# Seven block products in place of eight in half of the last matrix's contraction, with partial sums added by DMA and the residual kept in DRAM

## The chip, the core and the metric

One core of a Trainium2 chip runs the whole kernel. Its time is the device time of one execution in microseconds (us); the number compared is the median of several executions. Five engines work side by side, each through its own list of instructions in order: PE (TensorE, the matmuls), DVE (VectorE), ACT (ScalarE), POOL (GpSimd) and SP (SyncE, which here only issues transfers). They meet at semaphores. An instruction that waits holds up everything behind it on its own engine.

## The reference

One decoder layer on 256 positions with 2048 channels, all in float32:

```
u   = rms_norm(x)
o   = diff_attention(q, k, v of u)  +  conv module(u),  each times a sigmoid gate of u
h   = x + rms_norm(o @ w_out)
ff  = square(relu(rms_norm(h) @ w_ff1)) @ w_ff2      # 2048 -> 8192 -> 2048
out = h + rms_norm(ff)
```

The change is in the last product, `@ w_ff2`: 256 rows, a contraction over 8192, 2048 columns.

## The kernel before

**Precision.** Every weight and activation is kept as a rounded part (hi) and the rest (lo), both in the type float32r. A product is three matmuls: hi by hi, hi by lo, lo by hi. All weights come from DRAM as chunks of 128 x 2048 float32 (1 MB), loaded on SP's queue into `raw`. ACT casts a chunk to `wh` (L103), and DVE subtracts to get `wl` (L109). There are three buffers each of `raw`, `wh` and `wl`. `done()` after a chunk's last matmul frees a pair of `wh`, `wl`, and `fill()` then writes down the load and the split of the chunk three further on, so the cast of chunk i+3 waits for the last matmul of chunk i.

**Two ways to multiply.** `ws_pair` (L175 to L184) holds a piece of weight on PE and streams the activations: per chunk 16 matmuls of 512 columns and 16 of 256. `as_part` and `as_block` (L190 to L215) hold a piece of activation and stream the weight: per chunk 4 x 2 x 3 = 24 matmuls of 512 columns.

**Stages.** The convolution's input product runs to about 240 us, the heads with q, k, v and attention to 530, gates, convolution output and `w_out` to 840. Then comes the feed-forward part in four quarters q of its 8192 middle channels: 16 chunks of `w_ff1` with `ws_pair` (16 groups of middle channels are squared and split into the tiles `g`), then 16 chunks of `w_ff2` with `as_block`, for each of four blocks n of 512 columns four chunks kc. The sums of a block land in two PSUM banks and are copied to `acc` by ACT in quarter 0 (L658) and added to it by DVE afterwards (L660). Two tiles `ps` of two banks each take turns; four more banks (`psx`) serve everything else.

**Start.** The first two chunks are multiplied while they arrive. Meanwhile ACT and DVE form the squares of x, PE sums them over the partitions into `aux`, and ACT and DVE make `rb`, the row factors 1/rms (L217 to L219, called at L347). Every convolution pair's sum `z` (two buffers) is multiplied by `rb` at L391, so until `rb` is there the sums are parked in `z` and the PSUM tiles behind them stay full.

**Order of work.** A scheduler lays each engine's list out from the program text, its priorities (`high_priority`) and its own estimates, except where `pin` keeps program order. So an edit in one place can move instructions elsewhere.

Of the kernel before, what the change touches and what calls it, by code (L numbers as in the profile page):

```python
# [18 lines left out]
P = 128  # L19
# [26 lines left out]
EARLY = 3  # L46

# [5 lines left out]
def tile_layer(ctx, tc, x, x_t, pre, vecs, lams, rope_t, subln, b_conv, post_mix, post_ff,  # L53
# [9 lines left out]
    psx = ctx.enter_context(tc.tile_pool(name="psx", bufs=1, space=PSUM))  # L63
# [11 lines left out]
    for q in range(NQ):  # L75
        order += [w_f1[q * KT + ct] for ct in range(KT)]
        order += [w_f2[n, q * 4 + kc] for n in range(NB) for kc in range(4)]
    queue = []
    state = {"next": 0, "live": 0}

    pin = tc.keep_in_program_order

    def load(pieces):
        i = state["next"]
        state["next"] += 1
        state["live"] += 1
        chunk = (rawp.tile([P, CHUNK], F32, name="raw"), whp.tile([P, CHUNK], F32R, name="wh"),
                 wlp.tile([P, CHUNK], F32R, name="wl"))
        for j in range(pieces):
            load_part(chunk, i, j, pieces)  # L90
        queue.append(chunk[1:])
        return chunk
# [19 lines left out]

    def fill():
        while state["live"] < WBUFS and state["next"] < len(order):
            pieces = 4 if state["next"] in (n_mix, n_mix + 1, n_mix + 3) else 1
            chunk = load(pieces)
            w = CHUNK // pieces
            for j in range(pieces):
                split_hi(chunk, j * w, (j + 1) * w)
                split_lo(chunk, j * w, (j + 1) * w)  # L120

# [39 lines left out]

    def new_ps():
        return psm.tile([P, 2, 512], F32, name="ps")
# [36 lines left out]
    def as_block(acts, stagger=False, apart=False):  # L200
        ps = new_ps()
        pss = [ps[:, 0], aux_ps()] if apart else [ps[:, t] for t in range(NT)]
# [58 lines left out]
    lead = [load(0) for i in range(2)]  # L261

# [6 lines left out]
    load_x(0, 2)  # L269
    load_w(1, 0, nc.scalar)  # L270
    load_w(0, 0)
    pin(nc.scalar.dma_start(gpre, pre))
# [4 lines left out]
    for j in range(2, 4):  # L277
# [15 lines left out]
    mask = const.tile([P, S], F32, name="mask")  # L293
    nc.gpsimd.memset(mask, 0.0)
    nc.gpsimd.affine_select(mask[:, P:S], mask[:, P:S], pattern=[[-1, P]], compare_op=ALU.is_ge,
                            fill=NEG_INF, base=0, channel_multiplier=1)

# [54 lines left out]
    rope_sb = const.tile([P, 2, S], F32, name="rope_sb")  # L352
    pin(nc.sync.dma_start(rope_sb, rope_t))
    sub8 = const.tile([P, VD], F32, name="sub8")
    pin(nc.sync.dma_start(sub8, subln.partition_broadcast(P)))
    lam_in = const.tile([P, 4, HD], F32, name="lam_in")
    pin(nc.sync.dma_start(lam_in, lams.partition_broadcast(P)))

# [6 lines left out]
    tmpp = mid.enter_context(tc.tile_pool(name="tmpp", bufs=2))  # L365
    y_all = lnp.tile([P, KT, S], F32, name="y_all")
# [197 lines left out]
    gpool = ctx.enter_context(tc.tile_pool(name="gpool", bufs=KT // 2))  # L564
    pmx = fin.tile([P, D], F32, name="pmx")
    nc.gpsimd.dma_start(pmx, post_mix.partition_broadcast(P))
    y_sb = fin.tile([P, NT, D], F32, name="y_sb")
    h_sb = fin.tile([P, NT, D], F32, name="h_sb")
    nc.gpsimd.dma_start(h_sb, x_r)
# [5 lines left out]
    for n in range(NB):  # L575
        ps = as_block(ma, apart=(n == NB - 1))
        ns = slice(n * 512, (n + 1) * 512)
        with tc.high_priority(offset=CHAIN if n == NB - 1 else 0):
            for t in range(NT):
                sq = fin2.tile([P, 512], F32, name="fsq")  # L580
# [14 lines left out]
    def square(t, n):  # L595
        sq = fin2.tile([P, 512], F32, name="fsq")
# [18 lines left out]
    with tc.high_priority(offset=CHAIN):  # L615
        third = load(4)
        pin(nc.vector.reciprocal(r1[:, 0:1], r1[:, 0:1]))
# [18 lines left out]
    pff = pmx  # L636
    nc.gpsimd.dma_start(pff, post_ff.partition_broadcast(P))
# [3 lines left out]
    r3 = fin.tile([P, NT], F32, name="r3")  # L641
    for q in range(NQ):
        ga = Act(gpool, "g")
        for j in range(KT // 2):
# [4 lines left out]
            gg = fin2.tile([P, 2, S], F32, name="gg")  # L649
            nc.vector.scalar_tensor_tensor(gg, z, 0.0, z, op0=ALU.max, op1=ALU.mult)  # L650
            ga.put_pair(j, gg)
        for n in range(NB):
            ps = as_block(ga, stagger=(q == NQ - 1 and n == NB - 1), apart=(q == NQ - 1 and n == NB - 1))
# [92 lines left out]
```

## Time and profile before

| | |
|---|---|
| median of 3 runs | 1552.69 us (1552.65 to 1554.11) |
| profiled execution, its own time | 1552.62 us |
| span of its profile | 1550.9 us |
| instructions | 19142 |
| mean granted TensorE clock | 0.998 |
| PE, DVE, ACT busy, share of the span | 99%, 72%, 46% |

The span runs from the first to the last instruction; 1.7 us of the execution's own time lie outside it. Busy shares say how much an engine worked, not whether the others waited for it: that is read from what its instructions waited for.

### The profile page before, as it was taken

Reading aid. Unit: us, or ns where it says so; the run is one execution under the profiler, and the core shown is the slowest. Engines: PE = TensorE matmul, PEld = TensorE weight load, DVE = VectorE, ACT = ScalarE, POOL = GpSimd, SP = SyncE. Lnnn points to the kernel's source line nnn. Section 1 sums busy time; section 2 is a strip of 40 time slices with the busy share of each in tenths; the row PEclk is TensorE's granted clock in tenths of the full one; section 3 lists DMA queues with packets and bytes.
Section 4 is the critical chain, followed back from the end, with each engine's and each line's share of the span. In section 5 each row is a group of like instructions: output and inputs, shape, how many; then the busy total and the mean of one; then the engine's idle time right before and its main releaser. Section 6 shows DMA issues by size and latency. Waiting matters only on the chain.

```text
span 1550.9 us, 19142 instructions
## 1 busy us (share of the span) xinstructions
PE 1537.6 (99%) x7830; PEld 1314.2 (85%) x7830; DVE 1116.3 (72%) x1399; ACT 717.4 (46%) x743; POOL 5.1 (0%) x28
## 2 busy tenths in 40 slices
PE   9999999999999999999999999999999999999997
PEld 8888888888888888888887888888888888888886
DVE  7999999999999997966546764456545664466554
ACT  7444454645555545733446443444333443344442
POOL 0000000000000000000000000000000000000000
PEclk9999999999999999999999999999999999999999
DMA  8655555454545555555754655555455555555552
GB/s 304 218 191 188 188 190 187 165 188 163 190 163 187 193 201 192 179 200 180 270 196 156 225 188 185 191 210 188 173 195 209 190 190 180 198 193 190 187 193 82
DMA packets 45143, 296.86 MB, mean 191 GB/s; under 512 B 5120, under 2 KB 5248, under 8 KB 10368
## 3 DMA queue, kind: packets, MB, share of 16 engines
q1 hardware_dynamic: 43920, 289.61, 52.9%
q0 software_dynamic: 704, 5.24, 0.8%
q8 instruction: 61, 1.00, 0.3%
q10 hardware_dynamic: 432, 0.79, 0.2%
q14 instruction: 26, 0.21, 0.0%
HBM read 293.53 MB, written 2.10 MB: 191 GB/s over the span
## 4 chain that ended last, share of the span: by engine, by line
PE 99%; DVE 1%; ACT 0%; issue 0%; POOL 0%; DVEq 0%; ACTq 0%; POOLq 0%
PE ps L180 29%; PE ps L196 16%; PE ps L197 16%; PE ps L198 16%; PE ps L182 15%; PE ps L168 1%; PE po L463 1%; PE ps L171 1%; PE s L435 0%; PE aux L299 0%; PE aux L197 0%; PE aux L196 0%; PE aux L198 0%; DVE y_sb L679 0%; PE s L434 0%; PE aux L557 0%
## 5 line engine op out<-in xcount | busy, mean ns | idle before, releaser
L109 DVE TENSOR_TENSOR wl<-raw,wh 128x2048 fp32r<-128x2048 f32 (+2 forms) x292 | 625.0, 2144 | 368.0 <-ACT wh L103 363.9
L103 ACT CAST wh<-raw 128x2048 fp32r<-128x2048 f32 (+2 forms) x292 | 522.0, 1793 | 716.5 <-PE ps L198 352.2
L180 PE MATMUL ps<-act,wh 128*128 128x512 f32 x1984 | 478.9, 392 | 0.1
L180 PEld LDWEIGHTS ps<-act,wh 128*128 128x128 f32 x1984 | 364.3, 188 | 70.7 <-PE ps L182 0.3
L182 PEld LDWEIGHTS ps<-act,wl 128*128 128x128 f32 x1984 | 256.6, 191 | 10.1
L182 PE MATMUL ps<-act,wl 128*128 128x256 f32 x1984 | 263.8, 284 | 0.0
L196 PE MATMUL ps<-wh,act 128*128 128x512 f32 x624 | 243.9, 391 | 0.0
L197 PE MATMUL ps<-wl,act 128*128 128x512 f32 x624 | 243.4, 390 | 0.0
L198 PE MATMUL ps<-wh,act 128*128 128x512 f32 x624 | 243.3, 390 | 0.0
L380 DVE SCALAR_TENSOR_TENSOR y_all<-c,vec,y_all 128x256 f32<-128x256 f32 x480 | 209.1, 479 | 0.0
L196 PE MATMUL ps<-wh,g 128*128 128x512 f32 x496 | 193.0, 389 | 0.0
L197 PE MATMUL ps<-wl,g 128*128 128x512 f32 x496 | 193.0, 389 | 0.0
L198 PE MATMUL ps<-wh,g 128*128 128x512 f32 x496 | 192.9, 389 | 0.0
L198 PEld LDWEIGHTS ps<-wh,act 128*128 128x128 f32 x624 | 117.1, 188 | 24.2
L196 PEld LDWEIGHTS ps<-wh,act 128*128 128x128 f32 x624 | 117.2, 188 | 24.1
L197 PEld LDWEIGHTS ps<-wl,act 128*128 128x128 f32 x624 | 117.2, 188 | 23.8
L198 PEld LDWEIGHTS ps<-wh,g 128*128 128x128 f32 x496 | 93.1, 188 | 19.4
L196 PEld LDWEIGHTS ps<-wh,g 128*128 128x128 f32 x496 | 93.1, 188 | 19.2
L197 PEld LDWEIGHTS ps<-wl,g 128*128 128x128 f32 x496 | 93.1, 188 | 19.1
L188 DVE TENSOR_TENSOR z<-z,ps 128x512 f32<-128x512 f32 x64 | 43.5, 679 | 0.0
L187 ACT COPY z<-ps 128x512 f32<-128x512 f32 x64 | 37.5, 586 | 2.4 <-PE ps L182 1.6
L660 DVE TENSOR_TENSOR y_sb<-ps,y_sb 128x512 f32<-128x512 f32 x23 | 14.9, 686 | 20.1 <-PE ps L198 20.1
(172 smaller groups left out, 687.5 us busy)
## 6 DMA issues: line engine op xcount, KB each, us to landing
raw<-in_w_f_dram SPq DMA_DIRECT2D x124, 1024.0 KB, 4.8
raw<-in_w_q_dram SPq DMA_DIRECT2D x16, 1024.0 KB, 4.9
raw<-in_w_k_dram SPq DMA_DIRECT2D x16, 1024.0 KB, 4.8
raw<-in_w_v_dram SPq DMA_DIRECT2D x16, 1024.0 KB, 4.8
raw<-in_w_ga_dram SPq DMA_DIRECT2D x16, 1024.0 KB, 4.8
raw<-in_w_gc_dram SPq DMA_DIRECT2D x16, 1024.0 KB, 4.8
raw<-in_w_co_dram SPq DMA_DIRECT2D x16, 1024.0 KB, 4.8
raw<-in_w_o_dram SPq DMA_DIRECT2D x16, 1024.0 KB, 4.8
```

Source lines behind the costliest of these rows:

```text
L103: i = nc.scalar.copy(wh[:, a:b], raw[:, a:b])
L109: i = (eng or nc.vector).tensor_sub(wl[:, a:b], raw[:, a:b], wh[:, a:b].bitcast(F32))
L168: a = nc.tensor.matmul(ps, wh[:, sl], acts.both(k), start=(k == 0), stop=False)
L171: b = nc.tensor.matmul(ps[:, S:], wl[:, sl], acts.hi(k), start=False, stop=(k == KT - 1))
L180: nc.tensor.matmul(ps[:, j], wh[:, k * P:(k + 1) * P], acts.both(k), start=(k == 0), stop=False)
L182: nc.tensor.matmul(ps[:, j, S:], wl[:, k * P:(k + 1) * P], acts.hi(k), start=False, stop=(k == KT - 1))
L187: nc.scalar.copy(dst, ps[:, :, S:])
L188: nc.vector.tensor_tensor(dst, dst, ps[:, :, 0:S], op=ALU.add)
L196: nc.tensor.matmul(ps, acts.hi(k, a, b), wh[:, sl], start=(k == 0), stop=False)
L197: nc.tensor.matmul(ps, acts.hi(k, a, b), wl[:, sl], start=False, stop=False)
L198: nc.tensor.matmul(ps, acts.lo(k, a, b), wh[:, sl], start=False, stop=(k == KT - 1))
L380: i = nc.vector.scalar_tensor_tensor(y, c[:, j:j + S], vcol(ct, V_DW + j), y, op0=ALU.mult, op1=ALU.add)
```

## The change

**Products.** For seven of the eight pairs of column blocks (all but the second pair in quarter 3; `fast(q, m)`), the chunks kc 0 and 1 of both blocks are multiplied by blocks. The activations of a chunk form 2 x 2 blocks of 128 x 256, the weights of the two blocks of columns 2 x 2 blocks of 256 x 512, and seven products of sums of them take the place of the eight plain ones (Strassen's scheme): 42 matmuls per kc and pair in place of 48. kc 2 and 3 stay plain. The order of the four is `FF_ORDER` = 0, 2, 1, 3. The weight sums are formed by `fast_part` in four parts that carry 12, 12, 12 and 6 matmuls: per kc seven casts of 1024 columns on ACT (L159), seven subtractions (L160) and four additions (L165) of 1024 columns on DVE, in place of two casts and two subtractions of 2048. Both `raw` buffers of the pair stay taken until the fourth part. The activation sums are formed by `put_fast` for the first four groups of each quarter.

**Sums.** A pair of blocks uses all eight PSUM banks (`psx` is closed after the second norm and its banks become the pool `psy`). The scheme's own four banks are drained in mid-pair (one ACT copy, L798, four DVE additions, L800 to L803), the plain ones at the pair's end (four DVE additions, L819 to L822). In quarter 0 they go to `acc` directly, later to a tile `ev` (one buffer), which two DMAs per pair add to `acc` in SBUF (L825): ten DMAs of 512 KB over the five pairs.

**Residual.** `h_sb` (2 MB) is written to a DRAM tensor `h_keep` after the second norm (L730), and its SBUF goes to the new tiles; in quarter 3 it is read back in four pieces (L860), with the last gain (L857).

**Also moved.** `rope_sb`, `sub8`, `lam_in` and `mask` go to another pool, and their loads stand earlier on SP's queue: three rows from 13 on, ahead of a weight chunk, and not three rows from 23 on. The load of `gpre` comes first on ACT's queue, ahead of a weight piece.

```diff
+FAST = 2
+FF_ORDER = (0, 2, 1, 3)
+def fast(q, m):
+    return q < NQ - 1 or m == 0
...
+    def split_sum(wt, half, src):
+        hi, lo = (w[:, half * 1024:(half + 1) * 1024].rearrange("p (a n) -> p a n", a=2) for w in wt)
+        nc.scalar.copy(hi, src)
+        nc.vector.tensor_sub(lo, src, hi.bitcast(F32))
...
+        if part == 0:
+            split_sum(wt, 0, w11)
+            split_sum(wt, 1, new_sum("t1", w11, w12))
+            add(w12, w12, w22)
+        elif part == 1:
+            split_sum(wt, 0, w12)
+            split_sum(wt, 1, new_sum("t2", w12, w11))
+        elif part == 2:
+            split_sum(wt, 0, w21)
+            split_sum(wt, 1, new_sum("t4", sums["t2"], w21))
+        else:
+            split_sum(wt, 0, w22)
+            release_raw(i)
+            release_raw(i + 1)
...
-    load_w(1, 0, nc.scalar)
-    load_w(0, 0)
-    pin(nc.scalar.dma_start(gpre, pre))
+    pin(nc.scalar.dma_start(gpre, pre))
+    load_w(0, 0)
+    load_w(1, 0, nc.scalar)
...
-    rope_sb = const.tile([P, 2, S], F32, name="rope_sb")
-    pin(nc.sync.dma_start(rope_sb, rope_t))
...
+    rope_sb = lnp.tile([P, 2, S], F32, name="rope_sb")
+    pin(nc.sync.dma_start(rope_sb, rope_t))
...
+    nc.gpsimd.dma_start(h_keep, h_sb)
+    hst.close()
+    psx_st.close()
...
+        for kc in FF_ORDER:
+            if kc < FAST:
+                for pair in ((A1, A5), (A7, A6), (A2, A4), (A3,)):
+                    wh, wl = take()
+                    for half, a in enumerate(pair):
+                        ps = own[a] if a in own else shared[a]
+                        for i in range(2):
...
+                            nc.tensor.matmul(ps, g[:, 0, a], wh[:, sl], start=first, stop=False)
+                            nc.tensor.matmul(ps, g[:, 0, a], wl[:, sl], start=False, stop=False)
+                            nc.tensor.matmul(ps, g[:, 1, a], wh[:, sl], start=False, stop=last)
+                    done()
...
+        if q:
+            for t in range(NT):
+                nc.gpsimd.dma_start(acc[:, t, m * 1024:(m + 1) * 1024], ev[:, t].rearrange("p i n -> p (i n)"),
+                                    accum_op=ALU.add)
```

ACT's list at the start of the program, around the two instructions that make the row factors `rb` and `rt` from PSUM. Before:

```order
L187 COPY z<-ps 128x512 [waits PE_49]
L103 CAST wh<-raw 128x2048 [waits DMAHW4_49,PE_49]
L103 CAST wh<-raw 128x2048 [waits DMAHW5_49,DVE_49,PE_49]
L218 ACTIVATE rb<-aux,epsn 128x256 [waits PE_49]
L218 ACTIVATE rt<-aux,epsn 128x2 [waits PE_49]
L103 CAST wh<-raw 128x2048 [waits DMAHW6_49,DVE_49,PE_49]
L392 ACT_TABLE_LOAD [waits DMAHW0_49]
```

With the change:

```order
L278 COPY z<-ps 128x512 [waits PE_49]
L425 ACTIVATE xsq<-xt 128x1024 [waits DVE_49]
L143 CAST wh<-raw 128x2048 [waits DMAHW6_49]
L143 CAST wh<-raw 128x2048 [waits DMAHW7_49,PE_49]
L143 CAST wh<-raw 128x2048 [waits DMAHW0_49,DVE_49,PE_49]
L143 CAST wh<-raw 128x2048 [waits DMAHW1_49,DVE_49,PE_49]
L309 ACTIVATE rb<-aux,epsn 128x256 [waits PE_49]
L309 ACTIVATE rt<-aux,epsn 128x2 [waits PE_49]
```

From the second pair's copy to `rb`, two weight casts stood ahead, and now four do: one has slipped behind that copy, and one that came after `rb` now comes before it, where it waits for PE to free its buffer.

DVE's list at the same place, from the last addition of squares to the first product with `rb`. Before:

```order
L341 TENSOR_TENSOR xss<-xss 128x256 [waits DVE_49]
L109 TENSOR_TENSOR wl<-raw,wh 128x2048 [waits DMAHW5_49,PE_49,Activation_49]
L219 RECIPROCAL rb<-rb 128x256 [waits Activation_49]
L219 RECIPROCAL rt<-rt 128x2 [waits Activation_49]
L391 TENSOR_TENSOR z<-z,rb 128x512 [waits DVE_49]
L391 TENSOR_TENSOR z<-z,rb 128x512
```

With the change:

```order
L429 TENSOR_TENSOR xss<-xss 128x256 [waits DVE_49]
L149 TENSOR_TENSOR wl<-raw,wh 128x2048 [waits DMAHW0_49,PE_49,Activation_49]
L310 RECIPROCAL rb<-rb 128x256 [waits Activation_49]
L310 RECIPROCAL rt<-rt 128x2 [waits Activation_49]
L149 TENSOR_TENSOR wl<-raw,wh 128x2048 [waits DMAHW1_49,PE_49]
L482 TENSOR_TENSOR z<-z,rb 128x512 [waits DVE_49]
L482 TENSOR_TENSOR z<-z,rb 128x512
```

A weight subtraction now stands between the reciprocal and the products with `rb`.

PE's list in the feed-forward part, with buffer numbers, where one chunk of `w_ff2` follows another. Before, in quarter 1 (every chunk boundary there reads like this one):

```order
L197 MATMUL ps_8871<-wl_8805,g_8229 128x512
L198 MATMUL ps_8871<-wh_8804,g_8229 128x512
L196 MATMUL ps_8871<-wh_8834,g_8315 128x512 [waits Activation_49]
L197 MATMUL ps_8871<-wl_8835,g_8315 128x512 [waits DVE_49]
L198 MATMUL ps_8871<-wh_8834,g_8315 128x512
```

With the change, in the second pair of quarter 1, at the end of kc 1 and the start of kc 3 (`wh_9265` is the second part's buffer, `wh_9297` the third's, `wh_9317` the fourth's, `wh_9337` and `wh_9355` the two plain chunks'):

```order
L795 MATMUL ps_9166<-wh_9265,gs_8521 128x512
L794 MATMUL ps_9167<-wl_9298,gs_8432 128x512 [waits DVE_49]
L795 MATMUL ps_9167<-wh_9297,gs_8432 128x512
L793 MATMUL ps_9167<-wh_9297,gs_8521 128x512
L794 MATMUL ps_9167<-wl_9298,gs_8521 128x512
L795 MATMUL ps_9167<-wh_9297,gs_8521 128x512
L794 MATMUL ps_9168<-wl_9318,gs_8432 128x512 [waits DVE_49]
...
L795 MATMUL ps_9168<-wh_9317,gs_8521 128x512
L815 MATMUL ps_9167<-wh_9337,g_8785 128x512 [waits Activation_49]
L815 MATMUL ps_9168<-wh_9355,g_8785 128x512 [waits Activation_49]
L816 MATMUL ps_9167<-wl_9338,g_8785 128x512 [waits DVE_49]
```

The last matmul of the second part (first row) is now followed by only ten others before the first plain chunk's first matmul, and the second plain chunk's first matmul stands right behind that one, ahead of the first chunk's other 23.

## Rows read from the trace of the kernel before

**Rows 1.** The page's head and its busy times: us, share of the span, instructions.

```profile
span 1550.9 us, 19142 instructions
PE 1537.6 (99%) x7830; PEld 1314.2 (85%) x7830; DVE 1116.3 (72%) x1399; ACT 717.4 (46%) x743; POOL 5.1 (0%) x28
```

**Rows 2.** The chain of work that ended last, by engine.

```profile
PE 99%; DVE 1%; ACT 0%; issue 0%; POOL 0%; DVEq 0%; ACTq 0%; POOLq 0%
```

**Rows 3.** PE's waits: releaser, us in total, times, longest.

```profile
PE aux L299 <- POOL ident masks.py:199: 1.6, 1, 1.6
PE aux L236 <- DVE h_sb L592: 1.5, 2, 1.3
PE ps L168 <- DVE act L158: 0.4, 1, 0.4
```

**Rows 4.** Stretches: length, busy us by engine (instructions), clock, DMA share, GB/s.

```profile
753.00:766.00 13.00, 13.00 (x59) 10.77 (x58) 5.81 (x4) 7.38 (x6) 1.23 (x2) 1.00 0.96 399
1102.00:1189.00 87.00, 87.00 (x386) 72.03 (x385) 43.22 (x26) 30.01 (x18) 0.00 (x0) 1.00 0.53 187
```

**Rows 5.** Groups, 1102 to 1189: busy us, mean ns; idle before, releaser.

```profile
L109 DVE TENSOR_TENSOR wl<-raw,wh 128x2048 fp32r<-128x2048 f32 x16 | 36.7, 2293 | 40.9 <-ACT wh L103 40.9
L103 ACT CAST wh<-raw 128x2048 fp32r<-128x2048 f32 x16 | 30.6, 1913 | 52.9 <-PE ps L198 49.8 <-issue 3.1
L660 DVE TENSOR_TENSOR y_sb<-ps,y_sb 128x512 f32<-128x512 f32 x6 | 3.9, 686 | 3.6 <-PE ps L198 3.6
```

**Rows 6.** Timeline, w_ff2's start in quarter 1: start us, length us.

```profile
1100.23 1.91 ACT L103 CAST wh<-raw 128x2048 fp32r<-128x2048 f32 x1 [3.15 <-issue]
1101.90 0.40 PE L196 MATMUL ps<-wh,g 128*128 128x512 f32 x1
...
1102.17 2.29 DVE L109 TENSOR_TENSOR wl<-raw,wh 128x2048 fp32r<-128x2048 f32 x1 [2.67 <-ACT wh L103]
...
1104.38 0.68 DVE L188 TENSOR_TENSOR z<-z,ps 128x512 f32<-128x512 f32 x1
```

**Rows 7.** PE's timeline where quarter 2 begins.

```profile
1188.97 0.62 PE L180 MATMUL ps<-act,wh 128*128 128x512 f32 x2
```

**Rows 8.** Groups of the whole span, DVE and ACT, shapes apart.

```profile
L514 DVE TENSOR_TENSOR y_all<-y_all,acc 128x1024 f32<-128x1024 f32 x4 | 4.6, 1220 | 0.0
...
L337 ACT ACTIVATE xsq<-xt 128x1024 f32<-128x1024 f32 x3 | 3.1, 1051 | 0.0
...
L658 ACT COPY y_sb<-ps 128x512 f32<-128x512 f32 x8 | 4.2, 583 | 0.0
```

**Rows 9.** Timeline around `rb`.

```profile
46.14 0.47 ACT L218 ACTIVATE rb<-aux,epsn 128x256 f32<-128x256 f32 x1 [2.74 <-PE aux L343]
...
46.64 1.75 DVE L219 RECIPROCAL rb<-rb 128x256 f32<-128x256 f32 x1 [0.89 <-ACT rb L218]
...
47.98 1.91 ACT L103 CAST wh<-raw 128x2048 fp32r<-128x2048 f32 x1 [1.22 <-PE ps L180]
...
48.43 1.29 DVE L391 TENSOR_TENSOR z<-z,rb 128x512 f32<-128x512 f32 x2
...
53.56 0.29 DVE L412 TENSOR_SCALAR sub<-sub 128x256 f32<-128x256 f32 x1
...
53.77 0.42 DVE L406 TENSOR_TENSOR sq<-lam_in 128x256 f32<-128x256 f32 x1
...
54.75 0.68 DVE L188 TENSOR_TENSOR z<-z,ps 128x512 f32<-128x512 f32 x1
...
55.57 3.87 PE L180 MATMUL ps<-act,wh 128*128 128x512 f32 x16
```

**Rows 10.** DMA issues: queue, count, KB each, us from issue to landing.

```profile
raw<-in_w_f_dram SPq DMA_DIRECT2D x124, 1024.0 KB, 4.8
...
h_sb<-in_x_dram POOLq DMA_DIRECT2D x1, 2048.0 KB, 11.9
...
pmx<-in_post_ff_dram POOLq DMA_DIRECT2D x1, 1024.0 KB, 5.0
```

More of the change, by code (lines that the diff above doesn't have):

```diff
@@ L120, in fill @@
                 split_lo(chunk, j * w, (j + 1) * w)
+            release_raw(i)
     def take():
@@ new lines, in finish @@
+    def finish(n, t, dst, last):
+        sq = fin2.tile([P, 2, S], F32, name="z").rearrange("p a t -> p (a t)")
+        nc.scalar.activation(sq, dst, AF.Square, accum_out=fss[:, t, n:n + 1])
+        if last:
+            nc.scalar.activation(r3[:, t:t + 1], fss[:, t, n:n + 1], AF.Sqrt, bias=fpre[:, t:t + 1], scale=1.0 / D)
+        nc.vector.tensor_tensor(dst, dst, pff[n // 2][:, (n % 2) * 512:(n % 2 + 1) * 512], op=ALU.mult)
+        if last:
+            nc.vector.reciprocal(r3[:, t:t + 1], r3[:, t:t + 1])
@@ new lines, in tile_layer, with again @@
+        if q == NQ - 1:
+            def again():
+                return actp.tile([P, 2, 2 * S], F32R, name="act").bitcast(F32)
+            pff = [again().rearrange("p a n -> p (a n)") for i in range(2)]
+            for i in range(2):
+                nc.gpsimd.dma_start(pff[i], post_ff[i * 1024:(i + 1) * 1024].partition_broadcast(P))
+            h_fin = [again() for n in range(NB)]
+            for n in range(NB):
+                nc.gpsimd.dma_start(h_fin[n], h_keep[:, :, n * 512:(n + 1) * 512])
@@ new lines, in tile_layer @@
+        for m in range(NB // 2):
+            if fast(q, m):
+                fast_pair(ga, q, m)
+                if q == NQ - 1:
+                    for n in (2 * m, 2 * m + 1):
+                        for t in range(NT):
+                            finish(n, t, acc[:, t, n * 512:(n + 1) * 512], False)
+                continue
+            for n in (2 * m, 2 * m + 1):
+                last = n == NB - 1
+                ps = as_block(ga, stagger=last, apart=last)
+                for t in range(NT):
+                    dst = acc[:, t, n * 512:(n + 1) * 512]
@@ L672, in tile_layer @@
-            if q == NQ - 1 and n == NB - 2:
-                nc.vector.tensor_reduce(fpre, fss[:, :, 0:NB - 1], axis=AX.X, op=ALU.add)
-                nc.vector.tensor_scalar(fpre, fpre, 1.0 / D, NORM_EPS, op0=ALU.mult, op1=ALU.add)
+                        finish(n, t, dst, last)
+                if n == NB - 2:
+                    nc.vector.tensor_reduce(fpre, fss[:, :, 0:NB - 1], axis=AX.X, op=ALU.add)
+                    nc.vector.tensor_scalar(fpre, fpre, 1.0 / D, NORM_EPS, op0=ALU.mult, op1=ALU.add)
```

212 lines of the change are left out of this document (161 added, 51 removed).

## The prediction

> **What bounds the kernel now.** I read the page's busy times first: PE is busy 99% of a span of 1550.9 us [rows 1]. Busy can hide waiting, so the chain of waits came next: 99% of the chain that ended last is PE itself [rows 2], and all of PE's waits for another engine come to 3.5 us [rows 3]. So PE's own list sets the time, and a matmul taken out is worth its place in that list, if no new wait fills the place.
>
> Then the stage that is changed. In quarter 1 the 384 matmuls of `w_ff2` run from 1101.90 to 1188.97 [rows 6, 7]: 87.07 / 384 = 0.2267 us each (the 0.39 of one record overlaps the next). In that stretch PE is busy 87.0 of 87 us, DVE 43.2, ACT 30.0, and the DMA engines 0.53 [rows 4]. DVE and ACT sit idle until PE frees a buffer or ACT ends a cast [rows 5]. The reader is to see that the helpers have half of their time to spare here, and that nothing yet says how much they need at one moment.
>
> **What is removed.** Each changed pair loses 6 matmuls in each of two kc: 12. Seven pairs lose 84, and 84 x 0.2267 = **19.05 us**.
>
> **DVE and ACT in a changed pair.** PE now needs 180 x 0.2267 = 40.8 us a pair. DVE needs, per fast kc, 11 operations of 1024 columns. One lasts 1.22 [rows 8]; in a row they overlap by some 0.08, as the subtraction that starts at 1102.17 and its successor at 1104.38 do [rows 6]. So 11 x 1.18 = 13.0, twice 26.0; four plain chunks add 4 x 2.25 = 9.0 [rows 5], eight evictions 8 x 0.69 = 5.5 [rows 5]: **40.5 us of DVE against 40.8 of PE**. It was about half of that. On average DVE still fits, but it no longer has slack, and a fast kc alone asks 13.0 us of DVE in 42 x 0.2267 = 9.5 us of PE; the three buffers and the plain kc between them (10.9 us of PE, 4.5 of DVE) have to even this out. ACT needs 14 casts of 1.05, four of 1.91 and one copy of 0.58 [rows 5, 8], 23 us, and is not near its limit. Per quarter the activation sums add about 1.4 us of DVE in each of four groups, under the 16 chunks of `w_ff1`, where DVE also waits.
>
> **New waits at the hand-off.** A buffer is refilled by cast, then subtraction: 1.91, 0.03 of hand-off (the cast ends at 1102.14, the subtraction starts at 1102.17), 2.29 [rows 6]. Before, 48 matmuls or 10.9 us lie between a buffer's last matmul and its next use. Now parts have 12 and 6 matmuls. I walked each engine's list in order with these durations; two places stall.
>
> First, the plain chunk that follows a fast kc takes the buffer of the second part. Counted from the start T of that part's last matmul: it ends at T + 0.39, cast and subtraction follow, and with hand-offs of about 0.1 (PE resumes 0.14 after a DVE end, 55.43 to 55.57 [rows 9]) PE has `wl` at about T + 4.8. PE gets there after the third and fourth part (18 matmuls) and the chunk's first, at T + 20 x 0.2267 = 4.53. Stall 0.3. At the second and third such place in a quarter, one and two matmuls of the later parts have been drawn ahead, so that 17 and 16 lie between: 0.5 and 0.75.
>
> Second, the end of kc 1 in a quarter's second pair. PE's list shows the second plain chunk's first matmul directly behind the first chunk's, and the whole list waits for it. Both casts must be done in turn after the second part ends: T + 0.39 + 0.05 + 2 x 1.91 + 0.1 = T + 4.3, and PE is there at T + 12 x 0.2267 = 2.7. Stall 1.6, and 0.2 for the next `wl`. In quarter 0 17 matmuls lie between, but ACT's mid-pair copy also; 1.15. Quarter 3's only changed pair has the adjacent rows too.
>
> Sum: quarter 0 0.3 + 0.5 + 0.75 + 1.15 = 2.7; quarters 1 and 2 0.3 + 0.5 + 0.75 + 1.85 = 3.4 each; quarter 3 0.3 + 1.85 = 2.2: **11.7 us lost again**, 10.2 if every hand-off is as tight as 0.03.
>
> **The start.** The transfers that were moved have shifted the lists. In ACT's, a cast that waits for PE stands ahead of `rb`: 1.91 plus some 0.4 of waiting [rows 9] later. In DVE's, a subtraction of 2.29 stands between the reciprocal and the products with `rb`. Before, PE's next group of matmuls at 55.57 had just been released by the read of a PSUM sum that ended at 55.43, behind those products [rows 9]; PE had lost next to nothing. So a delay goes straight to PE: 2.3 + 2.2, less what no longer stands in between, since the work on `sub8` and `lam_in` (0.29 and 0.42 [rows 9]) has moved forward: **+3.7 us**. The earlier `gpre` may give back up to 0.8, which this wait swallows, since it ends by the row factors.
>
> **Accumulating DMAs.** No row shows one. As bounds: nothing, since they lie beside PE, and above that the nearest row, a copy of 1 MB in 5.0 us on POOL's queue [rows 10], here 1 MB per pair. `ev` is next written in mid-pair, 102 matmuls or 23 us later, less 3 us of evictions: up to four times the copy would be hidden from `ev`. What they take from the weight loads is 2.6 us per MB at the 399 GB/s that the row at 753 us shows when loads and POOL's transfers overlap; PE did not wait there (13.00 of 13.00 busy) [rows 4]. I take 0.5 us, bounds 0 and 2.
>
> The Trainium skill ("Collectives: The Full Stack", "The bandwidth ceiling: the fold count and why AG ≠ RS ≠ AR") says that an adding transfer reads two sources and so moves half as fast as a copy. By it the ten DMAs would take twice a copy's time, 10 us per pair, still hidden from `ev`; no run here shows it yet.
>
> The Trainium skill ("SBUF — State Buffer", "Who interferes with whom") also says that a transfer whose descriptors GpSimd makes can be starved by DVE, and that DVE operations with both inputs in SBUF do contend. That would work against this change, which keeps DVE at such operations nearly without a break; it is the second rival below. POOL's transfers at 753 us ran beside a DVE that was busy 5.81 of 13 us, so the trace doesn't decide it.
>
> **The rest at nothing.** `h_keep` (2 MB out and back) goes beside PE with the DMA engines at 0.53; its first user is a whole group later. The final additions read tiles of the same size from another place. If that cover were gone, the read back would cost its 2 MB, 11.9 us [rows 10], at the end.
>
> **Sum.** -19.05 + 11.7 + 3.7 + 0.5 = -3.15, and 1552.7 - 3.1 gives **1549.6 us**. The profiled execution's own time, 1552.62, is that of the median, 1552.69, so the sum stands against both.
>
> **Rivals.** (a) *More of the gain is kept.* If the hand-offs of the short parts are hidden (casts start earlier than I walked, or the drawn-ahead rows don't wait), up to 11.7 comes back, and the start's 3.7 likewise if ACT reaches `rb` sooner: 1538 to 1546. For it: the walk rests on three hand-offs of under 0.15. Against: the adjacency of the two rows is in PE's list, and a cast's 1.91 can't shrink.
>
> (b) *Adding transfers are slow.* If they land 20 us or more after issue, ACT's copy into `ev` waits, and the casts queued behind it on ACT; and as four copies they would take 10.5 us of all DMA engines per pair, when the next weight loads are due with some 8 us in hand. 2 to 3 us for each of five pairs, with a hard wait at two: +10 to +15, 1557 to 1565. It decides from about three times a copy.
>
> (c) *DVE becomes the bound.* 40.5 against 40.8 leaves 1%. If the additions, with strided or in-place operands, take 4% more than the row of 1024 columns, DVE is 1.6 us behind per pair, partly covered by `w_ff1`: by the walk +6 over seven pairs, 1555 to 1556. For it: no row shows such operands at this length. Against: the plain operations of 512, 1024 and 2048 columns, one of them reading PSUM, lie on one straight line (0.69, 1.22, 2.29) [rows 5, 8], so no form so far is dearer per column.
>
> (d) *Weight loads are late*, since both `raw` stay taken until the fourth part: two of three buffers are refilled at once, 4.8 us to the first landing [rows 10] and 2.6 to the next. At 399 GB/s it fits; at 340 the walk loses 6 us: 1555.
>
> **How the numbers follow.** A measurement of this kernel can tell 0.2% from no change, 3.1 us either way; 1549.6 lies on that edge. Forecast (1546.5 to 1552.5): 0.48; (a) 0.17; (b) 0.13; (c) 0.13; (d) 0.09. Faster by over 0.2%: (a) and half of the forecast, 0.42. Slower (above 1555.8): (b), and part of (c) and (d), 0.23. The rest 0.35. The range reaches into (a) and (b): 1543 to 1560.
>
> **What will show it.** Right: some 84 matmuls fewer; PE's waits at the lines that read the split weights of the plain chunks, L815 and L816, of 10 to 12 us in all, four to a quarter; a wait of 4 to 5 us near 59 us; PE busy between these. Wrong in direction (a): those waits under half as long. (b): ACT waiting at L798 for a DMA, or casts waiting for `raw`. (c): PE waiting for DVE at L794, with DVE at 9 tenths through `w_ff2`. (d): ACT waiting for `raw` at L159.

## The result, and the profile after

The changed kernel takes 1564.35 us (median of four runs, 1562.36 to 1565.78) against 1553.2 of the kernel before, measured beside it: a ratio of 1.007 (95% interval 1.0053 to 1.0088). It is **11 us slower**, where 3 us faster was forecast and 1543 to 1560 was the range.

The head and the busy times of the page of the changed kernel, and its chain of waits:

```profile
span 1563.4 us, 19364 instructions
PE 1530.4 (98%) x7746; PEld 1299.7 (83%) x7746; DVE 1272.5 (81%) x1609; ACT 769.1 (49%) x812; POOL 17.9 (1%) x44
PE 86%; DVE 6%; DMA 5%; ACT 2%; issue 1%; SPq 0%; DVEq 0%; ACTq 0%
```

Against [rows 1, 2] there are 84 matmuls fewer, as meant, and DVE is busy 156 us longer. What is new is the last line: the chain that was 99% PE now runs for 5% of the span through DMA, for 6% through DVE and for 2% through ACT. PE's waits, and ACT's waits for weights:

```profile
PE ps L815 <- ACT wh L143: 8.4, 6, 2.2
PE ps L271 <- DVE z L279: 4.6, 1, 4.6
PE ps L816 <- DVE wl L149: 4.0, 9, 1.0
PE ps L793 <- ACT wh L159: 2.0, 2, 1.1
PE aux L387 <- POOL ident masks.py:199: 1.6, 1, 1.6
PE aux L327 <- DVE h_sb L684: 1.5, 2, 1.3
...
ACT wh L143 <- DMA raw<-in_w_f_dram: 27.7, 9, 6.9
...
ACT wh L159 <- DMA raw<-in_w_f_dram: 7.6, 10, 1.8
```

The first, third and fourth line are the feed-forward part's new waits, the second is the start's, the next two were there before [rows 3]. The last two lines say what the prediction's sum did not have: ACT stands still 35 us for weights of the feed-forward part that have not landed (1.6 us before the change). Only what PE then waits for the casts costs time.

**Where the time went.** The stages are cut where the first matmul of `w_ff2` of each quarter starts, read from PE's timeline, in us; the kernels of the experiments stand in the same table. Each row is one execution, the profiled one.

```
                                    to w_ff2   quarter 0  quarter 1  quarter 2  rest
before                               925.79     176.11     176.11     176.11    96.75
changed                              932.85     177.21     178.42     177.49    97.43
e1  small loads later                926.39     175.34     176.61     177.88    98.54
e2  no adding DMAs                   935.47     174.16     173.61     174.61    97.20
e3  PE's list in program order       934.39     172.97     178.07     177.29    97.45
e4  no pair by seven products        932.86     176.11     176.10     176.11    96.57
e5  e1 + e2 + e3                     927.37     176.21     172.55     173.10   100.78
e6  e1 + e3, adding DMAs in halves   926.32     173.53     173.44     174.18    97.64
e7  e1 + e3                          927.16     173.08     177.88     177.21    97.28
e8  e1 + e3, GpSimd adds             926.68     173.91     176.20     177.72   101.41
e9  e6 + fourth raw buffer           926.25     172.11     172.13     172.46    94.54
e10 e7 + fourth raw buffer           928.14     172.12     173.04     173.52    94.58
e11 changed + fourth raw buffer      933.96     172.86     173.03     173.47    95.17
e12 e6 + e9's swaps of room          927.57     173.80     172.90     174.45    98.35
```

The start lost 7.06 us (forecast 3.7). A quarter without 24 matmuls should take 176.11 - 5.44 = 170.67, and the rest 96.75 - 2.72 = 94.03. So the three quarters lost 6.54, 7.75 and 6.82 and the rest 3.40: 24.5 us, where 11.7 and 0.5 for the adding DMAs had been put. The wait rows above show 14.4 of it. A row counts only the time in which no matmul is under way: of each of its 17 waits it misses 0.16 us (a record lasts 0.39, the place in the list 0.2267), and the second matmul behind a wait starts 0.34 after the first and not 0.2267; that is 0.27 x 17 = 4.6 more. Half clock, below, is another 3.1. Most of the last 2.4 are six gaps of 0.07 us in PE's timeline, too short for a wait row, that cost 0.34 each by the same reckoning.

**A wait for weights, step by step.** Stretches of the changed kernel in quarter 1, where the first pair ends and the second has begun; the columns are those of [rows 4], with the engines in the order PE, PEld, DVE, ACT, POOL:

```profile
1145.00:1150.00 5.00, 5.00 (x23) 4.13 (x23) 4.00 (x5) 1.33 (x2) 0.00 (x0) 1.00 0.56 220
1150.00:1155.00 5.00, 5.00 (x23) 4.13 (x22) 5.00 (x6) 3.64 (x4) 0.00 (x0) 1.00 0.00 0
1155.00:1160.00 5.00, 5.00 (x23) 4.01 (x22) 4.93 (x6) 3.06 (x3) 1.78 (x2) 1.00 0.80 131
1160.00:1165.00 5.00, 4.53 (x20) 3.42 (x20) 2.20 (x1) 0.00 (x0) 0.00 (x0) 1.00 0.99 301
1165.00:1170.00 5.00, 3.45 (x15) 2.32 (x13) 1.64 (x1) 2.95 (x2) 0.00 (x0) 1.00 0.97 409
1170.00:1173.50 3.50, 3.19 (x8) 2.21 (x8) 3.47 (x4) 0.54 (x1) 0.00 (x0) 0.51 0.45 147
```

and the timelines of POOL, DVE, SP and ACT in the same place:

```profile
1155.01 1.78 POOL L825 DMA_DIRECT2D y_sb<-ev  x2 [304.94 <-DVE ev L821]
...
1156.34 1.22 DVE L160 TENSOR_TENSOR wl<-raw,wh 128x1024 fp32r<-128x1024 f32 x1
...
1157.59 0.33 SPq L137 DMA_DIRECT2D raw<-in_w_f_dram  x1
...
1158.61 1.23 DVE L160 TENSOR_TENSOR wl<-raw,wh 128x1024 fp32r<-128x1024 f32 x1
...
1159.87 0.33 SPq L137 DMA_DIRECT2D raw<-in_w_f_dram  x1
...
1157.96 1.92 ACT L143 CAST wh<-raw 128x2048 fp32r<-128x2048 f32 x1 [1.82 <-PE ps L795]
1166.42 1.91 ACT L143 CAST wh<-raw 128x2048 fp32r<-128x2048 f32 x1 [6.55 <-DMA raw<-in_w_f_dram]
```

From 1150 to 1155 DVE is busy all the time and the DMA engines do nothing at all: two raw buffers belong to the fast kc, the third is full, and no load can start. They come free at 1157.56 and 1159.84, as the last subtractions that read them end, and loads follow at once (1157.59, 1159.87). But POOL has just sent off the two adding transfers (1155.01; their first packets move at 1156.45). The DMA engines are busy for 0.80 and then 0.99 of the next two stretches and move 131 and 301 GB/s, where the row with copies alone had 399 [rows 4]. The cast for the second plain chunk begins at 1166.42, after 6.55 us of waiting for its load, which took 8.8 us and not 4.8 [rows 10], and PE, whose list follows it, loses this:

```profile
1162.26 0.50 PE L816 MATMUL ps<-wl,g 128*128 128x512 f32 x1 [0.47 <-DVE wl L149]
...
1168.38 0.49 PE L815 MATMUL ps<-wh,g 128*128 128x512 f32 x1 [0.62 <-ACT wh L143]
1169.81 0.59 PE L793 MATMUL ps<-wh,gs 128*128 128x512 f32 x1 [0.93 <-ACT wh L159]
1170.71 0.79 PE L816 MATMUL ps<-wl,g 128*128 128x512 f32 x1 [0.31 <-DVE wl L149]
1171.30 0.63 PE L817 MATMUL ps<-wh,g 128*128 128x512 f32 x1
1171.73 0.63 PE L815 MATMUL ps<-wh,g 128*128 128x512 f32 x1
```

The last two rows show the second loss: matmuls that started 0.2267 apart now start 0.43 apart. The granted clock in the last stretch above is 0.51, that is 1.2 GHz and not 2.4, after a stretch in which PE had been busy 3.45 of 5 us. It stays there for 3.4 us. The profiled execution has three such places before its end, at 61, 1010 and 1170 us, each behind waits of PE, and each costs about 1.5 us of matmul time.

**The start.** Timelines of ACT, DVE and PE around `rb`, which answer to [rows 9]:

```profile
48.29 1.91 ACT L143 CAST wh<-raw 128x2048 fp32r<-128x2048 f32 x1 [3.66 <-PE ps L271]
50.10 0.47 ACT L309 ACTIVATE rb<-aux,epsn 128x256 f32<-128x256 f32 x1
...
52.30 2.27 DVE L149 TENSOR_TENSOR wl<-raw,wh 128x2048 fp32r<-128x2048 f32 x1
54.48 1.29 DVE L482 TENSOR_TENSOR z<-z,rb 128x512 f32<-128x512 f32 x2
...
61.16 5.07 PE L271 MATMUL ps<-act,wh 128*128 128x512 f32 x15 [4.57 <-DVE z L279]
```

The cast that waited for PE does stand ahead of `rb`, and the subtraction ahead of the products. `rb` comes 3.96 us later than before, the products 6.05, and PE resumes at 61.16 and not at 55.57: 5.6. Of that, 1.2 us was lost before: the first `ws_pair` matmul starts at 22.05 and not at 20.82. The three small tables are not shown to be the cause of this part, since with their loads moved away it starts at 21.76 in e1 and at 22.95 in e12; its cause stays open. Then the clock falls, 0.51 from 61 to 64.2 us, and adds 1.5.

### The profile page after: what moved, and what is told of

It is laid out like the page before. It is cut to its first block, busy times and chain, and to the rows that moved or that the text cites. A ratio compares the mean times of both kernels' runs of the same rounds, so it can differ in the third digit from the quotient of the medians.

```text
span 1563.4 us, 19364 instructions
## 1 busy us (share of the span) xinstructions
PE 1530.4 (98%) x7746; PEld 1299.7 (83%) x7746; DVE 1272.5 (81%) x1609; ACT 769.1 (49%) x812; POOL 17.9 (1%) x44
## 3 DMA queue, kind: packets, MB, share of 16 engines
q0 software_dynamic: 3008, 14.68, 3.7%
## 4 chain that ended last, share of the span: by engine, by line
PE 86%; DVE 6%; DMA 5%; ACT 2%; issue 1%; SPq 0%; DVEq 0%; ACTq 0%
PE ps L271 29%; PE ps L273 15%; PE ps L287 10%; PE ps L288 10%; PE ps L289 10%; DMA raw<-in_w_f_dram 4%; PE ps L816 2%; PE ps L817 2%; DVE wl L160 2%; PE ps L815 2%; DVE wl L149 2%; ACT wh L143 1%; DVE sum L165 1%; PE ps L793 1%; PE ps L795 1%; PE ps L794 1%
## 5 line engine op out<-in xcount | busy, mean ns | idle before, releaser
L143 ACT CAST wh<-raw 128x2048 fp32r<-128x2048 f32 (+2 forms) x264 | 467.8, 1780 | 550.2 <-PE ps L271 181.3
L149 DVE TENSOR_TENSOR wl<-raw,wh 128x2048 fp32r<-128x2048 f32 (+2 forms) x264 | 560.6, 2129 | 193.2 <-ACT wh L143 187.8
L815 PE MATMUL ps<-wh,g 128*128 128x512 f32 x224 | 89.0, 397 | 8.4 <-ACT wh L143 8.4
L816 PE MATMUL ps<-wl,g 128*128 128x512 f32 x224 | 90.2, 403 | 4.4 <-DVE wl L149 4.0
L159 ACT CAST wh<-raw 128x1024 fp32r<-128x1024 f32 x56 | 58.8, 1051 | 66.6 <-PE ps L271 26.7
L817 PE MATMUL ps<-wh,g 128*128 128x512 f32 x224 | 88.4, 395 | 0.0
L160 DVE TENSOR_TENSOR wl<-raw,wh 128x1024 fp32r<-128x1024 f32 x56 | 68.3, 1222 | 11.7 <-PE ps L273 10.8
L794 PE MATMUL ps<-wl,gs 128*128 128x512 f32 x196 | 76.4, 390 | 0.0
L795 PE MATMUL ps<-wh,gs 128*128 128x512 f32 x196 | 76.3, 389 | 0.0
L793 PE MATMUL ps<-wh,gs 128*128 128x512 f32 x196 | 72.9, 391 | 2.0 <-ACT wh L159 2.0
L159 ACT CAST wh<-sum 128x1024 fp32r<-128x1024 f32 x42 | 44.0, 1049 | 47.1 <-DVE sum L165 47.1
```

The costliest lines, as they stand in the source:

```text
L143: i = nc.scalar.copy(wh[:, a:b], raw[:, a:b])
L149: i = (eng or nc.vector).tensor_sub(wl[:, a:b], raw[:, a:b], wh[:, a:b].bitcast(F32))
L159: nc.scalar.copy(hi, src)
L815: nc.tensor.matmul(ps, ga.hi(k, a, b), wh[:, sl], start=first, stop=False)
L816: nc.tensor.matmul(ps, ga.hi(k, a, b), wl[:, sl], start=False, stop=False)
L817: nc.tensor.matmul(ps, ga.lo(k, a, b), wh[:, sl], start=False, stop=last)
```

## The experiments

Each result is a median with its ratio to the kernel before, measured beside it (95% interval).

**e1: the start put back.** The three loads are written down in the sixth pass of the convolution's loop; ACT's list at `rb` then reads as before the change.

```diff
+        if ct == 5:
+            pin(nc.sync.dma_start(rope_sb, rope_t))
+            pin(nc.sync.dma_start(sub8, subln.partition_broadcast(P)))
+            pin(nc.sync.dma_start(lam_in, lams.partition_broadcast(P)))
         ps = ws_pair(ua) if ct else lead_ps
```

> The changed kernel, with one thing put back: the loads of the three small tables are written down five convolution pairs later, so that the cast before the row factors stands where it stood before the change. My theory: the start costs the changed kernel about 7 us (4.7 of PE waiting for the row factors, 1.4 of half clock behind that wait, 1 of slower first loads), nothing of it given back later. So the first matmul of w_ff2 comes near 926 us, as before the change, and not at 932.9; the total falls by 6 to 7, to about 1557.5. Rival: the wait only shows a delay that comes from elsewhere in the changed program; then it moves on to the next pair and the total falls by less than 2.

1557.24 us, 1.0027 (1.0014 to 1.0039); `w_ff2` begins at 926.39. Of the start's 7.1 us 6.5 come back, nothing moves on, and the place of the small loads is their cause. The other 0.6 are what is left of the 0.9 that e1 loses before the first `ws_pair` matmul. The feed-forward part still loses.

**e2: no adding DMAs.**

```diff
-        if q:
-            for t in range(NT):
-                nc.gpsimd.dma_start(acc[...], ev[...], accum_op=ALU.add)
```

> The changed kernel without its ten adding DMAs: the sums of quarters 1 to 3 of the seven pairs never reach the accumulator, all else is as it was. My theory: the adding transfers run at the moment when both raw buffers of a pair come free and so push the next weight loads back; the waits of PE at about 1168 and 1347 us (2.6 and 3.1 us, and the half clock behind the first) go, quarters 1 and 2 get 3 to 4 us shorter each, the total falls by 6 to 8 to about 1557. Rival one: the loads are late because both raw buffers are held until DVE is done, the transfers hardly matter; then the total falls by less than 2. Rival two: DVE is the bound; then it stays.

1559.38 us, 1.0042 (1.0027 to 1.0057): 5.0 less, where 6 to 8 were expected. Quarters 1 and 2 fall by 4.8 and 2.9 us, near what the theory has. Quarter 0, which has no adding DMA in either kernel, also differs, by 3.0 (PE's longest wait there is 0.9 us here and 2.1 in the changed kernel), so not all of the difference is the transfers', and the first rival is not out.

**e3: PE's list of the changed pairs in program order.**

```diff
-                            nc.tensor.matmul(ps, g[:, 0, a], wh[:, sl], start=first, stop=False)
+                            pin(nc.tensor.matmul(ps, g[:, 0, a], wh[:, sl], start=first, stop=False))
```

(and the same for the other five matmul calls of `fast_pair`).

> The changed kernel with PE's list of the changed pairs held in the order of the program text, so that no matmul of a later part or chunk is drawn ahead. My theory, from the prediction: the waits of 1.5 to 2.3 us where the second plain chunk's first matmul stands behind the first chunk's go, the waits for the low part fall to 0.2 or 0.3 each, and the half clock at 1010 us goes with the wait ahead of it: the total falls by 7 to 9, to about 1556. Rival: the casts are late in any order, because their weights are loaded late; the waits then stand at the next matmul and the total falls by less than 2.

1562.38 us, 1.0062 (1.0046 to 1.0078): 2.0 less, where 7 to 9 were expected. Half and half: quarter 0 falls from 177.21 to 172.97, as expected; quarters 1 and 2 stay at 178.07 and 177.29, as the rival has it. There the drawn-ahead matmul only showed a cast that was late for its load: PE now waits 0.8 us at the high part and 1.8 at the low part of the same chunk.

**e4: the rest of the change alone.** `fast` returns False; plain blocks are copied in quarter 0 and added later.

```diff
 def fast(q, m):
-    return q < NQ - 1 or m == 0
+    return False
```

> The changed kernel with no pair multiplied by seven products: all chunks of w_ff2 plain, so no weight sums, no adding DMAs; the activation sums, the residual in DRAM, the four extra PSUM banks and the moved loads stay. My theory: what stays costs only the start's 7 us; each quarter takes 176.1 us as before the change, and the total is 1559 to 1560. Rival: the residual's way through DRAM or the activation sums cost something of their own; then the quarters are longer by 1 us or more.

1562.0 us, 1.0054 (1.0039 to 1.0069). The start is that of the changed kernel to 0.01 us, and the quarters are those of before to 0.01 us. The residual's way through DRAM, the activation sums and the four other PSUM banks cost nothing. The median is 2 us above the profiled run (1559.9) and above what was expected; its other runs have no profile, so that part stays open.

**e5: e1, e2 and e3 together.**

> Three things at once: the three small loads five pairs later (as in the first run), PE's list of the changed pairs in program order (as in the third), and the ten adding DMAs left out (as in the second), so that the sums of quarters 1 to 3 of the seven pairs are missing. My theory now: the row factors, the order of PE's list and the adding transfers are all that keeps the saved matmuls from showing. Then a quarter takes 172.5 to 173 us in place of 176.1, w_ff2 begins at 926.4, and the total is about 1542 to 1544, 10 below the kernel before. Rival: DVE or the held raw buffers bind by themselves; then the quarters stay at 174 or more and the total at 1547 or more.

1545.45 us, 0.996 (0.9946 to 0.9974), between the theory's 1542 to 1544 and the rival's 1547. Quarters 1 and 2 are at 172.55 and 173.10, as expected; but quarter 0, without any adding transfer, took 176.21 in the profiled run, with waits of PE of 1.4 and 1.8 us. That run, at 1552.17, is the longest of the five, and e6 and e7, whose program is the same in quarter 0, took 173.53 and 173.08 there, so the size of this loss is not typical. The stretches of that run in quarter 0:

```profile
945.00:950.00 5.00, 5.00 (x24) 4.14 (x23) 5.00 (x5) 3.58 (x4) 0.00 (x0) 1.00 0.01 3
950.00:955.00 5.00, 5.00 (x24) 4.14 (x23) 5.00 (x5) 4.18 (x5) 0.00 (x0) 1.00 0.18 38
955.00:960.00 5.00, 3.63 (x17) 2.70 (x15) 4.94 (x6) 2.46 (x2) 0.00 (x0) 1.00 0.93 354
960.00:965.00 5.00, 5.00 (x23) 4.13 (x22) 3.52 (x2) 1.21 (x2) 0.00 (x0) 1.00 0.93 280
```

The same pattern without transfers: 8 us in which nothing is loaded (945.7 to 954.0), then loads in a burst. So the held raw buffers are a cause of their own, and the transfers make it worse.

**e6 and e7: e1 and e3 with the adding DMAs, in halves and whole.** In e6 each pair has four of 256 KB, so that those of the first block of columns can go before the second is done:

```diff
-            for t in range(NT):
-                nc.gpsimd.dma_start(acc[:, t, m * 1024:(m + 1) * 1024], ev[:, t].rearrange("p i n -> p (i n)"),
-                                    accum_op=ALU.add)
+            for i in range(2):
+                for t in (1, 0):
+                    nc.gpsimd.dma_start(acc[:, t, (2 * m + i) * 512:(2 * m + i + 1) * 512], ev[:, t, i],
+                                        accum_op=ALU.add)
```

> The small loads later and PE's list in program order, and each pair's two adding DMAs of 512 KB cut into four of 256 KB, of which two can go when the first block of columns is drained, some 6 us before the others and while the DMA engines stand still. My theory: half of the collision with the next two weight loads goes; quarters 1 and 2 take 174 to 176 and the total is 1546 to 1550, faster than the kernel before. Rival: four adding transfers cost more than two (a fixed part each), so quarters 1 and 2 stay at 177 and the total at 1553.

> The small loads later and PE's list in program order, the two adding DMAs per pair as in the changed kernel. My theory: the start gives 6.5 back, quarter 0 takes 173, quarters 1 and 2 stay near 177, since the adding DMAs still push the loads back: total 1550 to 1553. Rival: with the waits for the casts gone the transfers find other gaps, and quarters 1 and 2 fall to 174: total 1547.

e6 takes 1547.76 us, 0.9964 (0.9951 to 0.9976), e7 1555.5, 1.0016 (1.0008 to 1.0025), which is 2.5 above what was expected of it. POOL's timeline at the first transfers, of e6 and then of e7:

```profile
1137.60 1.78 POOL L827 DMA_DIRECT2D y_sb<-ev  x2 [294.06 <-DVE ev L820]
1144.46 1.72 POOL L827 DMA_DIRECT2D y_sb<-ev  x2 [5.09 <-DVE ev L822]
...
1144.84 1.77 POOL L826 DMA_DIRECT2D y_sb<-ev  x2 [300.48 <-DVE ev L822]
```

Quarters 1 and 2 are 4.4 and 3.0 us shorter with the halves, of which some 3 are two stretches of half clock in e7 (at 1160 and 1338 us) that e6 doesn't have. The bytes are the same, and so is what they took of the DMA engines (3.7% of the span of all 16 in both): the place of the transfers makes most of their cost. Pieces of half the size go with it and were not tried without it. Both rivals fall.

**e8: GpSimd adds in place of the DMAs** (`nc.gpsimd.tensor_tensor` on `acc` and `ev`, four per pair).

> The small loads later and PE's list in program order, and the sums of quarters 1 to 3 added by four GpSimd additions of 512 columns per pair in place of the adding DMAs. My theory: the DMA engines are free for the weight loads, and GpSimd has nothing else to do, so quarters 1 and 2 take 173 to 174 and the total is 1543 to 1547. Rival: GpSimd and DVE hinder each other in reading SBUF; DVE's subtractions of 1024 columns beside the additions then last longer than 1.22 us, and with DVE near its limit the quarters stay at 176 or more.

1554.06 us, 1.0005 (0.9996 to 1.0014). The rival's mechanism shows. GpSimd's group over the whole span, DVE's groups from 1100 to 1200 us, and the timelines of GpSimd and DVE at the first two additions:

```profile
L828 POOL TENSOR_TENSOR y_sb<-y_sb,ev 128x512 f32<-128x512 f32 x20 | 41.5, 2099 | 540.0 <-DVE ev L820 526.8 <-DVE ev L822 13.2
...
L160 DVE TENSOR_TENSOR wl<-raw,wh 128x1024 fp32r<-128x1024 f32 x14 | 18.1, 1296 | 2.8 <-PE ps L273 2.4 <-ACT wh L159 0.3
L160 DVE TENSOR_TENSOR wl<-sum,wh 128x1024 fp32r<-128x1024 f32 x10 | 14.0, 1397 | 0.0
...
1138.09 3.54 POOL L828 TENSOR_TENSOR y_sb<-y_sb,ev 128x512 f32<-128x512 f32 x2 [294.19 <-DVE ev L820]
...
1138.52 1.95 DVE L165 TENSOR_TENSOR raw<-raw 128x1024 f32<-128x1024 f32 x1
1140.39 2.31 DVE L160 TENSOR_TENSOR wl<-sum,wh 128x1024 fp32r<-128x1024 f32 x1
```

DVE's operations on two SBUF tiles, 1.22 us otherwise, take 1.95 and 2.31 beside GpSimd's additions, and 1.30 and 1.40 on the mean of two groups in which most run alone. Quarters 1 and 2 are 2.8 and 3.5 us above those of e6. This execution, at 1557.7, is the longest of eleven, and two stretches of half clock (at 1149 and 1326 us) make about 3 of these 6.3 us, so what the hindrance costs by itself is not shown.

**e9 and e12: a fourth raw buffer, and its control.** Every fourth chunk of the feed-forward part goes to a buffer of its own. The room comes from the spare activation tile, which takes the sum t2, and from one scratch tile `sc` in place of two; e12 has these swaps and three buffers.

```diff
-            raws[i] = rawp.tile([P, CHUNK], F32, name="raw")
+            fourth = raw_x and i % 4 == 3
+            raws[i] = (raw_x[0] if fourth else rawp).tile([P, CHUNK], F32, name="raw")
...
-        while state["held"] < 3 and n_mix + 3 < state["raw"] < len(order):
+        while state["held"] < 3 + len(raw_x) and n_mix + 3 < state["raw"] < len(order):
...
+    raw_x.append(ctx.enter_context(tc.tile_pool(name="rawx", bufs=1)))
```

> The version with the small loads later, PE's list in program order and four adding DMAs per pair, and now a fourth raw buffer in the feed-forward part; its room comes from one scratch tile in place of two and a spare activation tile that takes the sum t2. My theory: while a fast kc is worked on, two of three raw buffers are held and no load can start, so that the next three loads come in a burst; with a fourth buffer the casts no longer wait for raw, only the 0.3 us behind the short parts stay, a quarter takes 172 us (176.11 less 24 x 0.2267 = 170.7, and four or five waits of 0.2 to 0.3) and the last stage 95: total 1541 to 1544. Rival: the adding transfers or DVE keep the quarters at 173.5 as with three buffers; total 1547.

> The control for the fourth buffer: the small loads later, PE's list in program order, four adding DMAs per pair, and the same swaps of room (one scratch tile, the spare activation tile), but three raw buffers. My theory: the swaps cost nothing, so the time is that of the earlier run with four adding DMAs, 1546 to 1549. Rival: the single scratch tile delays the activation sums; then it is 1 us or more slower, by a wait in the stage of w_ff1.

e9 takes **1539.26 us, 0.9913** (0.9899 to 0.9927), the fastest of all and 2 us below the lowest that was expected; e12 1548.55, 0.9969 (0.9958 to 0.998), as e6 within its spread (1545.35 to 1549.68). The swaps cost nothing that can be seen, and the buffer alone gives 9.3 us between the medians. In the profiled executions 8.3 of it lie in the four stages that the change touches, and 1.3 ahead of them, all of it before the first `ws_pair` matmul, long before the buffer is used. PE's and ACT's waits of e9, and in the last two lines ACT's of e12:

```profile
PE aux L389 <- POOL ident masks.py:199: 1.6, 1, 1.6
PE aux L329 <- DVE h_sb L687: 1.5, 2, 1.3
PE ps L261 <- DVE act L247: 0.6, 2, 0.4
PE ps L821 <- DVE wl L151: 0.4, 1, 0.4
PE ps L273 <- ACT wh L145: 0.3, 1, 0.3
...
ACT wh L145 <- DMA raw<-in_w_f_dram: 1.6, 1, 1.6
ACT wh L161 <- DMA raw<-in_w_f_dram: 1.0, 3, 0.4
...
ACT wh L143 <- DMA raw<-in_w_f_dram: 26.6, 12, 3.8
...
ACT wh L159 <- DMA raw<-in_w_f_dram: 8.9, 10, 1.9
```

ACT's waits for weights are 2.6 us in all, where e12 has 35.5 (26.6 and 8.9), and PE hardly waits in the feed-forward part. Neither of the two profiles shows half clock before the end, so the difference holds none of it.

**e10 and e11: the fourth buffer with the change's own transfers, and on the changed kernel alone.**

> As the run with a fourth raw buffer, but with the two adding DMAs of 512 KB per pair of the changed kernel. My theory: the adding transfers hurt only because no load was ahead; with a fourth buffer a load is ahead and the waits of 2 to 3 us in quarters 1 and 2 shrink to below 1, so quarters 1 and 2 take 172 to 174, total 1542 to 1546. Rival: the transfers delay any load by their own length; quarters 1 and 2 stay at 177 and the total is 1550 or more.

> The changed kernel with the fourth raw buffer alone: the start, PE's list and the two adding DMAs per pair as the change has them. My theory: the start keeps its 7 us, the drawn-ahead matmuls keep their waits of 1.5 to 2.3 us, the waits for raw go: quarters 0 to 2 at about 174 to 175, total 1556 to 1559 against 1564 with three. Rival: the raw buffers matter only behind the drawn-ahead matmuls; then less than 2 us is gained.

e10 takes 1543.18 us, 0.9937 (0.9924 to 0.995): quarters 1 and 2 at 173.04 and 173.52, so with a load in hand the whole transfers cost 1 us a quarter more than the halves (e9), and not 4.4 and 3.0 (e7 against e6). PE's longest wait for a split weight is 1.5 us, where less than 1 was expected. e11 takes 1550.74, 0.9982 (0.9973 to 0.9991), 13.6 below the changed kernel, with the start and the transfers as they were. It gained more than expected, and not all of it is the buffer's: with it the scheduler lays PE's list out anew, and the two first matmuls stand next to each other only in quarter 3, where PE waits 0.6 us.

## Why the prediction was wrong

- **The step that failed** is the sentence on the weight loads in rival (d), "At 399 GB/s it fits", and with it the 0.5 us for the adding DMAs. The walk let two loads land 4.8 and 2.6 us after their buffers came free, with the DMA engines to themselves, and so put PE's waits for weights at nothing in the sum. What binds is how many loads are in hand when a fast kc begins: with two of three buffers held by one kc, and DVE busy with its sums, nothing is loaded for 6 to 12 us, and then three loads and, in quarters 1 and 2, the transfers want the DMA engines together; the load issued at 1157.59 took 8.8 us. In the four stages the buffer alone is worth 8.3 us (e9 against e12; 9.3 between the medians), the place of the transfers 6.7 (e6 against e7; 7.7 between the medians).
- **Rival (b)** had half of the mechanism. ACT's copy into `ev` (L798) never waited for a transfer: they landed 4.6 to 11.0 us after their issue, and the one wait for them was 3.8 us of ACT at L830 in quarter 3, ahead of the squares of `acc`. Its other half came true, that the transfers take the DMA engines when the next loads are due, and so did its sign, casts that wait for `raw`. The chances were given to (b) and (d) one by one; they came together, and the transfers hurt because no load was in hand (e10). That 1564.35 lies in (b)'s 1557 to 1565 is in part luck, since the missing buffer, the order of PE's list and the start each added to it. What such a transfer costs: the queue of POOL took 1.7% of 16 engines' span for 9.44 MB in e2 and 3.7% for 14.68 MB in the changed kernel, so 31 us for 5.24 MB of adds, 6.0 us per MB, against 2.8 per MB for the copies between DRAM and SBUF. The two rows, of e2 and of the changed kernel:

```profile
q0 software_dynamic: 1568, 9.44, 1.7%
...
q0 software_dynamic: 3008, 14.68, 3.7%
```

  By the rule of the Trainium skill ("Collectives: The Full Stack", "The bandwidth ceiling: the fold count and why AG ≠ RS ≠ AR"), which the page states for the additions of a ReduceScatter, it would be twice; the trace agrees, at 2.1.
- **Rival (c), DVE's operations with strided or in-place operands**, did not come: 1.222 and 1.221 us in the groups of L160 and L165. That DVE has no slack mattered in another way: it sets when the raw buffers come free. The prediction took the rule of the Trainium skill ("SBUF — State Buffer", "Who interferes with whom") that DVE can starve GpSimd's transfers to work against this change. The same section says that `tensor_tensor`, the operation that DVE runs here, was not seen to stall a transfer. The trace agrees: in quarter 1 the first was issued at 1155.01, 0.3 us after the eviction that it waited for (L821, 1154.01 and 0.69 long), and its first packet moved 1.45 us later with DVE busy all the time; at 1202.44, with DVE busy for half of that time, it took 1.42.
- **The start** was the right mechanism, too small: 5.6 us of delay at the wait (1.2 of it lost before the first `ws_pair` matmul, where a gain or nothing had been put, and for a cause that stays open), and then 1.5 of half clock.
- **The hand-offs.** With loads in hand the walk holds: e9 loses 0.30 to 0.34 us behind the short parts where it puts 0.3, and e11, with one and two matmuls drawn ahead, 0.57 and 0.75 where it puts 0.5 and 0.75. The drawn-ahead matmuls cost 4.2 us in quarter 0 (e3), half clock included; in quarters 1 and 2 they only uncovered the late load.
- **The clock** was not in the sum at all. The chip granted 1.2 GHz in three stretches of 3.4 us behind waits: 4.6 us.

So of the feed-forward part's 24.5 us, about 8.3 are the missing buffer (the stages of e12 less those of e9), 6.7 the transfers' place (e7 less e6), 4.8 the drawn-ahead order (changed less e3), and 5 are the short waits that e9 still has. They were taken away one after the other, each figure comes from one execution of each kernel, and what one gives depends on the others. The clock's share follows the waits only in part and can't be separated here: of the 6.7, some 3 are half clock in e7.

## What to carry to other kernels

When a step needs two inputs at once and holds them longer, count the buffers at the moment it begins, not the bandwidth over its length: a stretch with the DMA engines at 0.00 ahead of a burst, and behind it a cast that waits for its load, is the sign. The stretch alone is not: e9 has the DMA engines at 0.00 from 1090 to 1100 us, and no cast waits for a load behind it. A transfer that is hidden on average should leave while the DMA engines are idle; cutting it in two, so that half could leave 3 to 7 us earlier (e6), took most of its cost away. And a table load of a few hundred KB, moved for its memory, can move a cast past the one instruction for which PE waits: compare the orders where a row sum or norm is made.

## What was not expected of the hardware

- The granted clock fell to 0.5 for 3.4 us in three places of the changed kernel: behind one wait of PE of 4.6 us (at 61 us), behind one of 2.1 (at 1010), and behind waits of 0.6 and 0.9 within 2 us (at 1170). It did not fall behind the wait of 2.2 us in quarter 3 at 1499 us. In other kernels it fell at other places (833, 1160 and 1338 us in e7, nowhere before the end in e9).
- Adding DMAs within SBUF moved their bytes at 2.1 times the cost of copies between DRAM and SBUF on the same queue.
- GpSimd's additions of 512 columns took 2.10 us, DVE's 0.69. Beside them DVE's operations with two SBUF inputs went from 1.22 us to 1.95 and 2.31, while those that read PSUM and one SBUF tile and ran partly beside them (L821 at 1137.92 and L823 at 1146.64 in e8) took 0.68 and 0.67. The Trainium skill ("SBUF — State Buffer", "Who interferes with whom") says just this of DVE's operations with two SBUF inputs and with one beside a GpSimd instruction that reads SBUF.
